# One PSUM pool with banks handed out in turn, and two reorderings around the norms, in a two-layer decoder trunk

## The chip, the core and the metric

The kernel runs on one core of a Trainium2 chip. The metric is the device time of one execution in microseconds (us). The core has five engines with a queue each: TensorE (PE, matmuls and transposes), VectorE (DVE), ScalarE (ACT), GpSimd (POOL) and SyncE (SP, which here issues the loads). Matmuls write to PSUM, which has eight banks of 128 x 512 f32; the other engines read the results from there. Each engine runs its instructions in the order of its queue.

## What is computed

The reference is a decoder trunk of two layers on x of 256 tokens by 1024 features, batch 1, all in f32:

```python
for i in range(DEPTH):
    h = rmsnorm(x, norm_mix[i])
    if i % 2 == 0:
        x = x + even_mixer(h, ...)   # 8 softmax heads and 16 Mamba-2 SSD heads, one projection in, one out
    else:
        x = x + gdn_mixer(h, ...)    # gated DeltaNet: conv, chunked delta rule, gated norm
    h = rmsnorm(x, norm_ffn[i])
    x = x + conv_ffn(h, ...)         # silu(conv(h @ w_gate) + b) * (h @ w_up) @ w_down
    x = x + per_layer_embedding(x, p[i], ...)  # sigmoid(rmsnorm(x) @ w_gate) * (p @ w_proj)
```

## The kernel before

Everything lies transposed in SBUF: features on the 128 partitions, the 256 tokens along the free axis, so that x is eight tiles of 128 x 256. A projection is made from blocks of 128 x 128 weights. `piece` (L133) loads 128 x 1024 weights (512 KB) through four buffers and splits them into a high half `whi` (ACT, L163) and a low half `wlo` (DVE, L164), each with four buffers of its own. `mm3` (L183) then runs three fp32r matmuls per block (L188 to L190): high times high, high times low, low times high. Activations are split likewise: `norm_tile` makes the halves `xx` of a tile of x (`split`, L217 on ACT and L218 on DVE) and the square of the tile (L241 on ACT), which POOL adds up to `nss` (L248). `norm_end` reduces the squares over the partitions on PE (`nps`, L255 and L256), turns them into 1/sqrt by a chain of eleven small DVE instructions (`st` L258, then `rsqrt`), and PE replicates the result over the partitions (`rep`, L270).

The stages follow each other: `even` (to about 192 us), `ffn(0)` with its per-layer embedding `ple` (to 402), `odd` (to 704), `ffn(1)` with its `ple` (to the end). The names in the rows: `pdt`, `pxbc`, `pz`, `pqk`, `pv` are projections of even, `pwa` its output projection; `rows`, `pxT`, `pyT` and the tiles `E` belong to the eight tiles of its SSD heads (function `ssd`), each of which takes on ACT six passes over 128 x 128 (L532 to L534, two heads) and two exponentials over 128 x 384 (L535). `pss` (L569) collects the sums of squares of q and k over the four passes of `qk`, and is read once, at L582. `psc` and `ppT` belong to its softmax heads, `pzs` to its group norm. `pg`, `pu`, `pd` are the FFN's projections, `pgt` the gate of `ple`, whose result `pleg` is made on DVE (L353, L355), ACT (tanh, L354) and added to x (L356). `pab` is odd's first projection, `pgd` its conv projections. For each of its eight key heads odd runs `prep` (a chain of small matmuls and copies: `rows`, `pS`, six times `pY` and `pST`, then `pR`, `pC` twice) and `core` (from `py0` on), while `pgd`, `pvT` and `pz` of other heads stand between them.

The Tile framework orders the instructions: each gets a priority by its place in the program, `high_priority(offset)` moves the ones inside it ahead by so many places, and a scheduler with its own durations sets each engine's queue by these and by when operands and buffers are there. The weight splits have an offset of 80 (`AHEAD`).

Of the eight PSUM banks one belongs to the pool `nrm` for the whole program. The other seven are opened stage by stage as a pool (`psum`, L114): `even` has 3 banks for `acc`, 2 for `ssd` and 2 for `att`; an FFN has 7 for `acc`; `odd` has 3 for `acc`, 1 for `core`, 2 for `prep0`, 1 for `prep1`. A tile of a kind gets a buffer of its kind, and the pool of the next stage is opened when that of the last is closed: the first tile of the new one waits until all of the old one's tiles have been read.

Of the kernel before, what the change touches and what calls it, by code (L numbers as in the profile page):

```python
# [7 lines left out]
F32 = mybir.dt.float32  # L8
# [4 lines left out]
ALU = mybir.AluOpType  # L13
# [3 lines left out]
P = 128  # L17
BLK = 1024
WARM = 30
WO = 7  # L20
AHEAD = 80
KICK = 2
T = 256
D = 1024
# [27 lines left out]
class Trunk:  # L52
    def __init__(self, ctx, tc, stream, xT, pT, pv, tok, cst, out):
        self.tc, self.nc, self.ctx = tc, tc.nc, ctx
        self.stream, self.out = stream, out
        self.off = 0
        self.order = []
        self.n = 0
        self.pshare, self.share = 0.0, 0.0
        nc = self.nc  # L60
        ep = ctx.enter_context
        self.cpool = ep(tc.tile_pool(name="cpool", bufs=1))
        self.rawp = ep(tc.tile_pool(name="rawp", bufs=4))
        self.splp = ep(tc.tile_pool(name="splp", bufs=4))
        self.smallp = ep(tc.tile_pool(name="smallp", bufs=3))
        self.chain = ""
        self.nrm = ep(tc.tile_pool(name="nrm", bufs=1, space=PSUM))

        self.xx = self.moving(self.cpool, 2 * KD, "xx")
        warm = self.cpool.tile([P, 1], F32, tag="warm", name="warm")  # L70
        nc.vector.memset(warm, 0.0)
        nc.scalar.activation(warm, warm, AF.Exp)

        zt = self.cpool.tile([P, 256], F16, tag="zt", name="zt")
        nc.vector.memset(zt, 0.0)
        pz = self.nrm.tile([P, 512], F32, tag="nrm", name="pwarm")
        for _ in range(WARM):
            nc.tensor.matmul(pz[:, :T], zt[:, :P], zt, start=True, stop=True)
        self.pv = self.cpool.tile([P, NPV], F32, tag="pv", name="pv")
        nc.scalar.dma_start(self.pv, pv)  # L80
        xs = self.cpool.tile([P, KD, T], F32, tag="x", name="x")
        for m in range(0, KD, 2):
            nc.sync.dma_start(xs[:, m:m + 2], xT[:, m:m + 2])
        self.x = [xs[:, m] for m in range(KD)]
        self.tok = self.cpool.tile([P, 64], F32, tag="tok", name="tok")
        self.cst = self.cpool.tile([P, NCC], F32, tag="cst", name="cst")
        self.cst_src, self.tok_src = cst, tok
        self.pT = pT
        self.ones = self.cpool.tile([P, 1], F32, tag="ones", name="ones")
        nc.gpsimd.memset(self.ones, 1.0)  # L90
        self.ident = self.c("ident")
        self.id16 = self.cpool.tile([P, P], F16, tag="id16", name="id16")
        self.zb = [[self.cpool.tile([P, 4, P], F16, tag=f"zb{s}_{l}", name=f"zb{s}_{l}") for l in range(6)]
                   for s in range(1)]
# [19 lines left out]
    @contextmanager  # L114
    def psum(self, **banks):

        assert sum(banks.values()) <= 7
        with self.tc.tile_pool(name=self.uid("psum"), bufs=1, space=PSUM) as pool:
            self.psp, self.banks = pool, banks
            yield  # L120

    def acc(self, s="acc"):
        return self.psp.tile([P, 512], F32, tag="acc", name=self.uid(s), bufs=self.banks["acc"])

    def sm(self, s="sm"):
        if self.chain in self.banks:
            return self.psp.tile([P, 512], F32, tag=self.chain, name=self.uid(s), bufs=self.banks[self.chain])
        return self.nrm.tile([P, 512], F32, tag="nrm", name=self.uid(s))

    def small(self, n, s="st", dt=F32):  # L130
# [79 lines left out]
    def split(self, src, hi, lo, scale=None):  # L210

        nc = self.nc
        if scale is None:
            nc.scalar.activation(hi, src, AF.Copy)
            nc.vector.tensor_tensor(lo, src, hi.bitcast(F32), op=ALU.subtract)
        else:
            nc.scalar.activation(hi, src, AF.Copy, scale=scale)  # L217
            nc.vector.scalar_tensor_tensor(out=lo, in0=src, scalar=scale, in1=hi.bitcast(F32),  # L218
                                           op0=ALU.mult, op1=ALU.subtract)


    def norm_begin(self, gain, pool=None):
# [28 lines left out]
    def norm_end(self):  # L251
# [3 lines left out]
            nc.tensor.matmul(ps[:, c:c + 1], self.nss[:, c * P:(c + 1) * P], self.ones, start=True, stop=False)  # L255
            nc.tensor.matmul(ps[:, c:c + 1], self.nlast[:, c * P:(c + 1) * P], self.ones, start=False, stop=True)  # L256
        t = self.small(2)
        nc.vector.tensor_scalar(out=t, in0=ps[:, 0:2], scalar1=1.0 / D, scalar2=EPS, op0=ALU.mult, op1=ALU.add)  # L258
        r = self.cpool.tile([P, 2], F32, tag="rtok", name=self.uid("rtok"), bufs=2)
        self.rsqrt(t, 2, r)  # L260
        self.r = r
# [79 lines left out]
    def ple(self, i, nxt, pool):  # L341
# [4 lines left out]
        for m0 in range(0, KD, 2):  # L346
            ws = self.piece([("ple_w_gate", i, 0, KD, (m0 + j) * P, P) for j in range(2)])
            for j in range(2):
                m = m0 + j
                ps = self.acc("pgt")  # L350
                self.mm3(ps[:, :T], ws[j], a)
                g = pool.tile([P, T], F32, tag="pleg", name=self.uid("pleg"), bufs=4)
                nc.vector.tensor_tensor(g, ps[:, :T], self.R, op=ALU.mult)  # L353
                nc.scalar.activation(g, g, AF.Tanh, scale=0.5)  # L354
                nc.vector.scalar_tensor_tensor(out=g, in0=g, scalar=1.0, in1=self.pp[m], op0=ALU.add, op1=ALU.mult)  # L355
                nc.vector.tensor_tensor(self.x[m], self.x[m], g, op=ALU.add)  # L356
                if nxt:
                    self.norm_tile(m)
                else:
                    nc.sync.dma_start(self.out[:, m], self.x[m])  # L360
        if nxt:
            self.norm_end()

# [789 lines left out]
```

## Time and profile before

| | |
|---|---|
| time, three runs | 919.47, 921.43, 921.58 us (median 921.43) |
| the profiled execution's own time, its span | 923.28 us, 921.5 us |
| PE busy | 900.1 us, 98% |
| PE weight loads | 860.1 us, 93% |
| DVE busy | 747.3 us, 81% |
| ACT busy | 584.8 us, 63% |
| POOL busy | 42.9 us, 5% |
| mean granted PE clock | 0.992 of full speed |

The span is the time from the first to the last instruction that the profiler saw, the time of the execution stands a little above it. PE is busy nearly all the time, so PE's idle time and its clock are what is left to look at. Full speed is 2.4 GHz; a granted clock of 0.5 is the lower of the two levels, 1.2 GHz.

### The profile page before, as it was taken

Reading aid. Unit: us, or ns where it says so; the run is one execution under the profiler, and the core shown is the slowest. Engines: PE = TensorE matmul, PEld = TensorE weight load, DVE = VectorE, ACT = ScalarE, POOL = GpSimd, SP = SyncE. Lnnn points to the kernel's source line nnn. Section 1 sums busy time; section 2 is a strip of 40 time slices with the busy share of each in tenths; the row PEclk is TensorE's granted clock in tenths of the full one; section 3 lists DMA queues with packets and bytes.
Section 4 is the critical chain, followed back from the end, with each engine's and each line's share of the span. In section 5 each row is a group of like instructions: output and inputs, shape, how many; then the busy total and the mean of one; then the engine's idle time right before and its main releaser. Section 6 shows DMA issues by size and latency. Waiting matters only on the chain. (4 is left out here: it accounts for less than half of the span.)

```text
span 921.5 us, 19977 instructions
## 1 busy us (share of the span) xinstructions
PE 900.1 (98%) x7834; PEld 860.1 (93%) x7834; DVE 747.3 (81%) x1662; ACT 584.8 (63%) x1237; POOL 42.9 (5%) x53
## 2 busy tenths in 40 slices
PE   8999999999999999999989999999999999999997
PEld 6988778999999999989889999999999999999997
DVE  6977778988888767789979998999868888876665
ACT  6577555667565545667678778787755665554552
POOL 0000112110000001010000000000002000000100
PEclk9999999999999999999989999999999999999999
DMA  7534332466666566545413333432345666666571
GB/s 276 181 122 131 93 114 92 140 197 193 203 186 197 177 203 209 169 138 158 141 47 93 114 100 108 119 113 88 122 134 177 184 194 199 190 193 189 179 227 48
DMA packets 40990, 141.40 MB, mean 153 GB/s; under 512 B 4672, under 2 KB 6208, under 8 KB 40896
## 3 DMA queue, kind: packets, MB, share of 16 engines
q1 hardware_dynamic: 40608, 139.84, 48.6%
q8 instruction: 61, 1.00, 0.4%
q10 hardware_dynamic: 288, 0.29, 0.1%
q14 instruction: 33, 0.27, 0.1%
HBM read 139.06 MB, written 1.05 MB: 152 GB/s over the span
## 5 line engine op out<-in xcount | busy, mean ns | idle before, releaser
L163 ACT ACTIVATE whi<-raw 128x1024 fp32r<-128x1024 f32 (+2 forms) x266 | 277.7, 1044 | 176.8 <-PE pd L189 38.6
L164 DVE TENSOR_TENSOR wlo<-raw,whi 128x1024 fp32r<-128x1024 f32 (+2 forms) x266 | 319.8, 1202 | 81.8 <-ACT whi L163 79.7
L188 PE MATMUL pg<-xx,whi 128*128 128x256 f32 x352 | 97.4, 277 | 0.6 <-DVE x L703 0.3
L188 PE MATMUL pu<-xx,whi 128*128 128x256 f32 x352 | 97.5, 277 | 0.0
L189 PE MATMUL pg<-xx,whi 128*128 128x256 f32 x352 | 97.4, 277 | 0.0
L189 PE MATMUL pu<-xx,whi 128*128 128x256 f32 x352 | 97.4, 277 | 0.0
L190 PE MATMUL pu<-xx,wlo 128*128 128x256 f32 x352 | 97.4, 277 | 0.0
L190 PE MATMUL pg<-xx,wlo 128*128 128x256 f32 x352 | 97.2, 276 | 0.0
L188 PE MATMUL pd<-yy,whi 128*128 128x256 f32 x352 | 97.2, 276 | 0.0
L189 PE MATMUL pd<-yy,whi 128*128 128x256 f32 x352 | 97.2, 276 | 0.0
L190 PE MATMUL pd<-yy,wlo 128*128 128x256 f32 x352 | 97.2, 276 | 0.0
L188 PE MATMUL pgd<-xx,whi 128*128 128x256 f32 x256 | 76.1, 297 | 0.4 <-DVE z L989 0.4
L190 PE MATMUL pgd<-xx,wlo 128*128 128x256 f32 x256 | 75.0, 293 | 0.0
L189 PE MATMUL pgd<-xx,whi 128*128 128x256 f32 x256 | 74.8, 292 | 0.0
L188 PEld LDWEIGHTS pg<-xx,whi 128*128 128x128 f32 x352 | 66.1, 188 | 0.8 <-issue 0.8
L188 PEld LDWEIGHTS pu<-xx,whi 128*128 128x128 f32 x352 | 66.1, 188 | 0.0
L189 PEld LDWEIGHTS pu<-xx,whi 128*128 128x128 f32 x352 | 66.1, 188 | 0.0
L190 PEld LDWEIGHTS pu<-xx,wlo 128*128 128x128 f32 x352 | 66.1, 188 | 0.0
L189 PEld LDWEIGHTS pg<-xx,whi 128*128 128x128 f32 x352 | 66.1, 188 | 0.0
L190 PEld LDWEIGHTS pg<-xx,wlo 128*128 128x128 f32 x352 | 66.1, 188 | 0.0
L188 PEld LDWEIGHTS pd<-yy,whi 128*128 128x128 f32 x352 | 66.1, 188 | 0.0
L189 PEld LDWEIGHTS pd<-yy,whi 128*128 128x128 f32 x352 | 66.1, 188 | 0.0
(357 smaller groups left out, 2636.1 us busy)
## 6 DMA issues: line engine op xcount, KB each, us to landing
raw<-stream SPq DMA_DIRECT2D x232, 512.0 KB, 3.6
raw<-stream SPq DMA_DIRECT2D x32, 448.0 KB, 3.3
x<-xT SPq DMA_DIRECT2D x4, 256.0 KB, 4.9
out<-x SPq DMA_DIRECT2D x8, 128.0 KB, 1.9
cst<-cst SPq DMA_DIRECT2D x1, 645.0 KB, 7.1
raw<-pT SPq DMA_DIRECT2D x2, 256.0 KB, 2.5
pv<-pv ACTq DMA_DIRECT2D x1, 215.5 KB, 4.4
raw<-stream SPq DMA_DIRECT2D x1, 128.0 KB, 2.0
```

What stands on the lines that cost most here:

```text
L163: nc.scalar.activation(hi, raw[:, :cols], AF.Copy)
L164: self.lo_engine(lo).tensor_tensor(lo_, raw[:, :cols], hi.bitcast(F32), op=ALU.subtract)
L188: nc.tensor.matmul(out, wh, ah, start=start and k == 0, stop=False)
L189: nc.tensor.matmul(out, wh, al, start=False, stop=False)
L190: nc.tensor.matmul(out, wl, ah, start=False, stop=stop and k == n - 1)
```

## The change

It has three parts. One pool `banks` of seven tiles, `bank0` to `bank6`, is kept for the whole program. `psum` now gives each kind of tile a list of banks, those least recently handed out first, and `bank` hands a kind's banks out in strict turn. In `ple`, what follows the gate matmuls of the last two tiles (m = 6, 7) is put into a `high_priority` of 400, `LAST`. In `norm_end` the instruction `st` is issued only after the last low half of an `xx` tile (`lastlo`).

```diff
@@ -19,6 +19,7 @@
 WARM = 30
 WO = 7
 AHEAD = 80
+LAST = 400
 KICK = 2
 T = 256
 D = 1024
@@ -65,6 +66,8 @@
         self.smallp = ep(tc.tile_pool(name="smallp", bufs=3))
         self.chain = ""
         self.nrm = ep(tc.tile_pool(name="nrm", bufs=1, space=PSUM))
+        self.psp = ep(tc.tile_pool(name="banks", bufs=1, space=PSUM))
+        self.used = [0] * 7
 
         self.xx = self.moving(self.cpool, 2 * KD, "xx")
         warm = self.cpool.tile([P, 1], F32, tag="warm", name="warm")
@@ -114,17 +117,25 @@
     @contextmanager
     def psum(self, **banks):
 
+        free = sorted(range(7), key=lambda b: self.used[b])
         assert sum(banks.values()) <= 7
-        with self.tc.tile_pool(name=self.uid("psum"), bufs=1, space=PSUM) as pool:
-            self.psp, self.banks = pool, banks
-            yield
+        self.banks = {}
+        for kind, n in banks.items():
+            self.banks[kind], free = free[:n], free[n:]
+        yield
+
+    def bank(self, kind, s):
+        b = self.banks[kind].pop(0)
+        self.banks[kind].append(b)
+        self.used[b] = self.n
+        return self.psp.tile([P, 512], F32, tag=f"bank{b}", name=self.uid(s))
 
     def acc(self, s="acc"):
-        return self.psp.tile([P, 512], F32, tag="acc", name=self.uid(s), bufs=self.banks["acc"])
+        return self.bank("acc", s)
 
     def sm(self, s="sm"):
         if self.chain in self.banks:
-            return self.psp.tile([P, 512], F32, tag=self.chain, name=self.uid(s), bufs=self.banks[self.chain])
+            return self.bank(self.chain, s)
         return self.nrm.tile([P, 512], F32, tag="nrm", name=self.uid(s))
 
     def small(self, n, s="st", dt=F32):
@@ -215,8 +226,8 @@
             nc.vector.tensor_tensor(lo, src, hi.bitcast(F32), op=ALU.subtract)
         else:
             nc.scalar.activation(hi, src, AF.Copy, scale=scale)
-            nc.vector.scalar_tensor_tensor(out=lo, in0=src, scalar=scale, in1=hi.bitcast(F32),
-                                           op0=ALU.mult, op1=ALU.subtract)
+            self.lastlo = nc.vector.scalar_tensor_tensor(out=lo, in0=src, scalar=scale, in1=hi.bitcast(F32),
+                                                         op0=ALU.mult, op1=ALU.subtract)
 
 
     def norm_begin(self, gain, pool=None):
@@ -255,7 +266,8 @@
             nc.tensor.matmul(ps[:, c:c + 1], self.nss[:, c * P:(c + 1) * P], self.ones, start=True, stop=False)
             nc.tensor.matmul(ps[:, c:c + 1], self.nlast[:, c * P:(c + 1) * P], self.ones, start=False, stop=True)
         t = self.small(2)
-        nc.vector.tensor_scalar(out=t, in0=ps[:, 0:2], scalar1=1.0 / D, scalar2=EPS, op0=ALU.mult, op1=ALU.add)
+        with self.tc.issue_after(self.lastlo.ins):
+            nc.vector.tensor_scalar(out=t, in0=ps[:, 0:2], scalar1=1.0 / D, scalar2=EPS, op0=ALU.mult, op1=ALU.add)
         r = self.cpool.tile([P, 2], F32, tag="rtok", name=self.uid("rtok"), bufs=2)
         self.rsqrt(t, 2, r)
         self.r = r
@@ -349,15 +361,16 @@
                 m = m0 + j
                 ps = self.acc("pgt")
                 self.mm3(ps[:, :T], ws[j], a)
-                g = pool.tile([P, T], F32, tag="pleg", name=self.uid("pleg"), bufs=4)
-                nc.vector.tensor_tensor(g, ps[:, :T], self.R, op=ALU.mult)
-                nc.scalar.activation(g, g, AF.Tanh, scale=0.5)
-                nc.vector.scalar_tensor_tensor(out=g, in0=g, scalar=1.0, in1=self.pp[m], op0=ALU.add, op1=ALU.mult)
-                nc.vector.tensor_tensor(self.x[m], self.x[m], g, op=ALU.add)
-                if nxt:
-                    self.norm_tile(m)
-                else:
-                    nc.sync.dma_start(self.out[:, m], self.x[m])
+                with self.tc.high_priority(offset=LAST if m >= KD - 2 else 0):
+                    g = pool.tile([P, T], F32, tag="pleg", name=self.uid("pleg"), bufs=4)
+                    nc.vector.tensor_tensor(g, ps[:, :T], self.R, op=ALU.mult)
+                    nc.scalar.activation(g, g, AF.Tanh, scale=0.5)
+                    nc.vector.scalar_tensor_tensor(out=g, in0=g, scalar=1.0, in1=self.pp[m], op0=ALU.add, op1=ALU.mult)
+                    nc.vector.tensor_tensor(self.x[m], self.x[m], g, op=ALU.add)
+                    if nxt:
+                        self.norm_tile(m)
+                    else:
+                        nc.sync.dma_start(self.out[:, m], self.x[m])
         if nxt:
             self.norm_end()
 
```

The numbers behind a name tell one tile from another; a line of "..." leaves out rows that repeat the one above them or the one below. The rows of the changed kernel have its own line numbers, 3 to 13 higher.

First place: PE in the even layer, around the `rows` of the second ssd tile. Before, they stand in the middle of the `pxbc` matmuls, one tile ahead of that tile's `pyT`:

```order
L188 MATMUL pxbc_161_815<-xx_1_70,whi_154_775 128x256
L415 MATMUL rows_144_739<-cst_115,ac_69_313 128x128 x2
L538 MATMUL pyT_141_721<-E_142_722,xd_140_719 64x256
L539 MATMUL pyT_141_721<-E_142_722,xd_140_719 64x128
L415 MATMUL rows_144_739<-cst_115,ac_69_313 128x128 x2
L189 MATMUL pxbc_161_815<-xx_1_70,whi_154_775 128x256
...
L523 MATMUL pxT_145_744<-cst_115,xbc1_124_633 128x128 x2
...
L190 MATMUL pqk_172_863<-xx_1_70,wlo_168_854 128x256
L538 MATMUL pyT_147_749<-E_148_750,xd_146_747 64x256
L539 MATMUL pyT_147_749<-E_148_750,xd_146_747 64x128
```

Now the same tile's `rows` and `pyT` (its names are `rows_143` and `pyT_146`) stand behind the last `pss`, among the `pv` matmuls:

```order
L201 MATMUL pqk_254_1322<-xx_1_73,wlo_250_1288 128x256
L620 MATMUL pv_292_1464<-whi_295_1468,xx_1_73 128x512
...
L582 MATMUL pss_108_552<-cst_118,sqk_256_1349 128x2 x2
L621 MATMUL pv_293_1465<-whi_295_1468,xx_1_73 128x512
...
L621 MATMUL pv_293_1465<-whi_295_1468,xx_1_73 128x512
L428 MATMUL rows_143_739<-cst_118,ac_68_313 128x128 x4
L622 MATMUL pv_293_1465<-wlo_296_1469,xx_1_73 128x512
...
L621 MATMUL pv_293_1465<-whi_298_1486,xx_1_73 128x512
L551 MATMUL pyT_146_749<-E_147_750,xd_145_747 64x256
L552 MATMUL pyT_146_749<-E_147_750,xd_145_747 64x128
L428 MATMUL rows_183_953<-cst_118,ac_68_313 128x128 x4
L551 MATMUL pyT_146_749<-E_148_758,xd_145_747 64x256
```

With them the same instructions of ssd tiles 2 to 7 have moved behind the last `pss`; 37 `pv` matmuls are left behind `rows_143`, of 48.

Second place: PE at the start of `odd`. Before, `pab` (24 matmuls) meets the first `nps` after 13 of them, and all the rest but three stand ahead of the first `pgd`:

```order
L190 MATMUL pab_1004_5463<-xx_1_70,wlo_1003_5460 32x256
L188 MATMUL pab_1004_5463<-xx_1_70,whi_1002_5459 32x256
L255 MATMUL nps_982_5409<-ones_116,nss_978_5373 128x1
L189 MATMUL pab_1004_5463<-xx_1_70,whi_1002_5459 32x256
```

Now 18 stand ahead of the first `nps`, and `pgd` follows behind the next one:

```order
L200 MATMUL pab_1001_5455<-xx_1_73,whi_999_5451 32x256
L201 MATMUL pab_1001_5455<-xx_1_73,wlo_1000_5452 32x256
L266 MATMUL nps_980_5405<-ones_119,nss_976_5369 128x1
L199 MATMUL pab_1001_5455<-xx_1_73,whi_999_5451 32x256
L199 MATMUL pgd_1039_5560<-xx_1_73,whi_1033_5549 128x256
```

The first matmul of `pab` follows the last `pgt` in both.

Third place: PE in `odd`, the end of the first head's chain (`pR`, `pC`) and the start of `core` (`py0`) and of the next `prep` (`pS`). Before, six and six `pgd` matmuls stand around the second `pR`, two behind the last `pC`, and none between `py0` and `pS`:

```order
L892 MATMUL pR_1101_5851<-nid_998_5451,id16_118 128x512
L189 MATMUL pgd_1321_6817<-xx_1_70,whi_1314_6805 128x256
...
L188 MATMUL pgd_1321_6817<-xx_1_70,whi_1314_6805 128x256
L899 MATMUL pR_1101_5851<-S32_1097_5832,L32_1077_5701 128x128 x4
L189 MATMUL pgd_1321_6817<-xx_1_70,whi_1314_6805 128x256
...
L904 MATMUL pC_1103_5859<-R16_1102_5857,T16_1082_5719 128x128
L189 MATMUL pgd_1321_6817<-xx_1_70,whi_1314_6805 128x256
L190 MATMUL pgd_1321_6817<-xx_1_70,wlo_1315_6806 128x256
L928 MATMUL py0_1216_6414<-bv_1203_6331,S32_1097_5832 128x128
L856 MATMUL pS_1165_6104<-id16_118,T16_1163_6101 128x128
```

Now the second `pR` runs without `pgd` in front, four stand behind it with `pvT`, and two, `rows` and three more lie ahead of `py0` and `pS`:

```order
L905 MATMUL pR_1098_5843<-nid_995_5443,id16_121 128x512
L912 MATMUL pR_1098_5843<-S32_1094_5824,L32_1074_5693 128x128 x4
L931 MATMUL pvT_1212_6401<-cst_118,v2_1207_6365 128x128 x2
L199 MATMUL pgd_1324_6850<-xx_1_73,whi_1314_6803 128x256
...
L199 MATMUL pgd_1324_6850<-xx_1_73,whi_1314_6803 128x256
L917 MATMUL pC_1100_5851<-R16_1099_5849,T16_1079_5711 128x128
...
L201 MATMUL pgd_1324_6850<-xx_1_73,wlo_1315_6804 128x256
L428 MATMUL rows_1281_6625<-cst_118,gc_1025_5532 128x128 x4
L199 MATMUL pgd_1324_6850<-xx_1_73,whi_1314_6803 128x256
...
L941 MATMUL py0_1213_6406<-bv_1200_6323,S32_1094_5824 128x128 x2
L869 MATMUL pS_1162_6096<-id16_121,T16_1160_6093 128x128
```

What moved is the fill between the steps of the chain, not the steps.

## Rows read from the trace of the kernel before

**Rows 1.** The page, busy us, share of the span, instructions.

```profile
PE 900.1 (98%) x7834; PEld 860.1 (93%) x7834; DVE 747.3 (81%) x1662; ACT 584.8 (63%) x1237; POOL 42.9 (5%) x53
```

**Rows 2.** PE's waits, whole span: us in total, times, longest.

```profile
PE pab L188 <- DVE pleg L353: 2.0, 1, 2.0
PE pS L856 <- DVE T L852: 2.0, 1, 2.0
PE rep L270 <- DVE ry L206: 1.4, 1, 1.4
...
PE pwa L188 <- DVE ri L196: 1.0, 1, 1.0
...
PE py L928 <- DVE S L905: 0.5, 1, 0.5
...
PE pvT L918 <- DVE v L384: 0.3, 1, 0.3
PE pg L188 <- DVE x L703: 0.3, 1, 0.3
...
PE nps L255 <- POOL nss L248: 0.3, 1, 0.3
```

**Rows 3.** Windows: busy us of PE, PEld, DVE, ACT, POOL; granted clock; DMA.

```profile
100.00:110.00 10.00, 10.00 (x54) 7.09 (x54) 8.09 (x24) 8.40 (x23) 0.95 (x1) 1.00 0.36 107
162.00:164.00 2.00, 2.00 (x19) 1.97 (x18) 1.95 (x4) 2.00 (x5) 0.00 (x0) 1.00 0.60 236
404.00:406.00 2.00, 1.76 (x11) 1.52 (x12) 2.00 (x4) 1.12 (x3) 0.58 (x1) 0.69 0.62 221
406.00:408.00 2.00, 2.00 (x12) 1.71 (x11) 1.62 (x6) 0.68 (x2) 0.15 (x1) 0.50 0.65 164
408.00:410.00 2.00, 2.00 (x19) 1.95 (x18) 0.16 (x1) 1.64 (x3) 0.00 (x0) 0.96 0.25 102
464.00:466.00 2.00, 2.00 (x19) 1.82 (x18) 1.44 (x5) 1.17 (x4) 0.00 (x0) 0.50 0.48 193
466.00:468.00 2.00, 2.00 (x13) 1.91 (x13) 0.39 (x2) 1.43 (x5) 0.00 (x0) 0.50 0.00 0
468.00:470.00 2.00, 2.00 (x16) 1.91 (x16) 1.05 (x4) 1.27 (x5) 0.00 (x0) 0.60 0.00 0
```

**Rows 4.** Timeline, 401 to 406: start, us, engine, line, tile, idle before.

```profile
401.95 0.28 PE L190 MATMUL pgt<-xp,wlo 128*128 128x256 f32 x1
...
402.47 0.95 DVE L218 SCALAR_TENSOR_TENSOR xx<-x,pv,xx 128x256 fp32r<-128x256 f32 x1
...
404.24 0.28 PE L188 MATMUL pab<-xx,whi 128*32 128x256 f32 x1 [2.01 <-DVE pleg L353]
...
404.36 0.28 PE L189 MATMUL pab<-xx,whi 128*32 128x256 f32 x1
...
405.42 0.73 POOL L248 TENSOR_TENSOR nss<-nss,nsq 128x256 f32<-128x256 f32 x1 [2.28 <-ACT nsq L241]
```

**Rows 5.** Timeline of PE, 100 to 106.

```profile
100.29 0.60 PE L415 MATMUL rows<-cst,ac 128*128 128x128 f32 x4
100.73 0.38 PE L523 MATMUL pxT<-cst,xbc 128*128 128x128 f32 x2
...
101.65 0.39 PE L607 MATMUL pv<-whi,xx 128*128 128x512 f32 x1
101.88 0.39 PE L608 MATMUL pv<-whi,xx 128*128 128x512 f32 x1
...
104.81 0.65 PE L538 MATMUL pyT<-E,xd 128*64 128x256 f32 x2
...
105.60 0.44 PE L523 MATMUL pxT<-cst,xbc 128*128 128x128 f32 x2
```

**Rows 6.** Lines of ACT, 40 to 155: busy, mean ns, idle before.

```profile
L163 ACT ACTIVATE whi<-raw 128x1024 fp32r<-128x1024 f32 x25 | 26.6, 1063 | 18.8 <-PE pqk L189 9.2 <-PE pv L608 5.3 <-PE pxbc L189 3.3
L535 ACT ACTIVATE E<-E 128x384 f32<-128x384 f32 x16 | 8.5, 530 | 0.1
...
L532 ACT ACTIVATE E<-rows,ac 128x128 f32<-128x128 f32 x16 | 5.9, 372 | 0.3 <-PE rows L415 0.2
```

## The prediction

> **What bounds the kernel now.** I read the page's busy shares first: TensorE (PE) is busy for 900.1 of the span's 921.5 us [rows 1]. So only two things can move the time: the some 20 us in which PE idles, and the stretches in which its granted clock is under 1. The amount of matmul work is the same before and after. Next come PE's waits [rows 2]: two of them are 2 us long, and both lie in the odd layer. The windows [rows 3] then show that each of these two holes is followed by a stretch at half the granted clock (0.50, the lower of its two levels, 1.2 GHz). That is a second price as large as the hole itself. The timeline shows who is late at the first hole [rows 4], and what PE and ScalarE (ACT) spend on one ssd tile in the even layer [rows 5, 6], where the change moves most instructions.
>
> My sum is made against the profiled execution's 923.28 us, 1.85 above the median 921.43 of the runs shown. I take the difference as it comes out and put it to the median. A measurement of this kernel tells 0.3%, or 2.8 us, from no change.
>
> **The start of odd (the pab matmuls).** The last pgt matmul starts at 401.95, and pab's first one at 404.24 [rows 4]: PE idles 2.0 us [rows 2] until VectorE (DVE) has read the old pool's last bank, because the new pool is opened as a whole. Then the clock drops: 2 us at 0.69, 2 at 0.50, 2 at 0.96 [rows 3] lose 2 x (0.31 + 0.50 + 0.04) = 1.7 us. Together 3.7 us. With banks handed over singly, pab's bank was read long ago. The order says that 18 pab matmuls (six of eight input tiles) now come first, some 0.118 us apart (404.24, 404.36 [rows 4]): PE is then busy from 402.1 to 404.2, and stands next at the first nps matmul, which needs the running sum of squares with tile 6. Before, that sum ended at 405.42 + 0.73 = 406.15 [rows 4]. In the new order tile 6's x add stands one 0.33 us instruction earlier on DVE, and its tanh ahead of the older tile's square on ACT, so about 405.8. A stall of 1.6 us replaces the hole. LAST does not bring more, since the 1.2 us weight split still stands ahead of m 7's chain in DVE's order. Does a 1.6 us stall drop the clock? The nearest rows are the 1.4 of rep [rows 2], which ends at 160.6 and after which the window from 162 still shows 1.00 [rows 3], and the 2.0 above. 1.6 is nearer to 1.4, so I take 3.7 - 1.6 = **2.0 gained**, and 0.4 for the bound where the clock drops all the same. The st instruction behind the last low half costs nothing here: that half (0.95 us beside a POOL add [rows 4]) no longer stands between st and the rest of the rsqrt, and PE has pgd matmuls to run, the wait for xx 7 being the longer one.
>
> **Middle of odd (455 to 470).** The holes py 0.5, pS 2.0 and pvT 0.3 [rows 2] come to 2.8 us, and the clock behind them loses 2 x (0.50 + 0.50 + 0.40) = 2.8 us in three windows [rows 3]. The two prep banks are now in strict turn, and the scheduler lays the same pgd fill differently: less between pR and pC, and some with rows and pvT ahead of py0 and pS. The chain pR, ACT copy, pC, DVE add is unchanged and there is as much fill, so I leave the idle time at 2.8 us, but in pieces of 0.4 to 1.2 us by the lengths of the steps. None reaches 1.4, so no clock drop: **2.8 gained**, with bounds of 0 (the clock still falls) and 4 (part of the idle goes too). Later a turn of the prep chain (pS to pY) has no fill left: **0.6 lost** (0 to 1.0), my estimate: two of the shorter waits of 0.3 [rows 2].
>
> **Even layer, ssd (45 to 118).** Here the turn costs something that the diff does not say. The tile pss is taken from the att kind and stays alive until all four qk passes have written it. Of the two att banks, round-robin gives every second rows tile pss's bank, so the rows of ssd tile 1 wait until pss was read, and with them, in order, everything of ssd tiles 1 to 7: rows, the E passes, pyT. Before, they lay among pxbc and pqk matmuls. Now they come behind the last pss, among the 37 pv matmuls left. Between two tiles' pyT PE has its own work of rows 0.44 (100.29 to 100.73), pxT about 0.26, two heads of pyT 1.58 (104.81 to 105.60 is one), four pv at 0.23 [rows 5]: 3.2 us. ACT needs six passes of about 0.37 and two of 0.53 [rows 6], 3.3 us by durations (they overlap, so some less). That is a near balance, where before PE was busy for 10.00 of 10 us [rows 3]. The first pyT also waits for rows, ACT and a DVE product in a row with a weight split (1.06 us [rows 6]) in front, about 1 us. I take 1.0 + 0.4 + five tiles at 0.15 = **2.2 lost**. The bounds are 0 (pv covers all) and 6 (each tile waits for a split of 1.06 too).
>
> **Attention and the group norm (118 to 168).** With its fill used up earlier, attention has some 88 pz matmuls to hide its softmax chains in where it had 133. I charge four waits like those that a chain leaves elsewhere (0.3 to 0.5 [rows 2]): **1.5 lost** (0 to 4). In return a block of 24 matmuls (2.8 us) now stands between the group norm's pzs and its rep, which idled 1.4 [rows 2]: **1.0 gained** (0 to 1.4). The pwa wait of 1.0 stays.
>
> **Stage changes to the two FFNs.** pg's waits of 0.3 for the first x and nps's 0.3 [rows 2] lie where nps and rep now come after 12 and 23 of the new stage's matmuls, not after 7 and 9: **0.9 gained** over both (0 to 1.6). DMAs, weight splits and their order on the SP queue are unchanged, and cost nothing.
>
> Sum: -2.0 - 2.8 + 0.6 + 2.2 + 1.5 - 1.0 - 0.9 = -2.4, so 923.28 becomes 920.9 and the median **919.0 us**.
>
> **Rivals.**
> *Stalls take the holes' place.* PE meets nps at 404.2 and the shorter stalls at 460 add up, and the clock falls to half as before. For it: the half clock follows both 2 us holes, and 1.6 lies between the rows. Against it: after 1.4 it did not fall. Then the two gains shrink to 0.4 and 0, the sum is +2.0, and the time 923.4. The Trainium skill (TensorE: Matmul & The Clock Gate, section "A second HAM failure mode: psum-queue depth-cycling") speaks for it: cycling through PSUM banks gave short idles between groups of matmuls, over which the clock swung. By that rule the time would be this case's 923.4, by the rows alone 919.0; no row of before shows whether short idles in a row do this here.
>
> *The squeezed ssd becomes the bound (slower).* Place: PE between the last pqk and the first psc, 100 to 118. If pz's weight splits (1.06 us [rows 6]) fall among the E passes, ACT has 4.4 us a tile against PE's 3.2. Five tiles then cost 1.2 each, with 1.0 for the first: 7.0 instead of 2.2. One of these stalls reaching 2 us brings a clock dip of 1.7 as at 402. The sum is then -2.4 + 4.8 + 1.7 = +4.1, or 925.5. It decides from some 5.2 us lost there above the 2.2 (for +2.8). For it: both engines are near balance. Against: the E passes overlap, and DVE (8.09 of 10 busy) and ACT (8.40) had room in the same stretch [rows 3].
>
> *Everything is covered.* ssd and attention stalls hide behind pv and pz, both clock drops and some of the idle go, and 1.0 of the 3.7 lost there is left: -2.0 - 4.0 - 1.0 - 0.9 + 0.6 + 1.0 = -6.3, or 915.1.
>
> **How the numbers follow.** Forecast 0.40, stalls in the holes' place 0.27, ssd the bound 0.19, everything covered 0.14. The forecast's 919.0 lies just inside 0.3%, so I give half of it (0.21) to faster and 0.19 to same. The second case is same but for 0.03 slower. So faster 0.21 + 0.14 = 0.35, same 0.19 + 0.24 = 0.43, slower 0.19 + 0.03 = 0.22. The forecast alone holds from 916.5 to 921.5. The range that leaves out one in five takes in nearly all of the two outer cases: 914.5 to 925.5.
>
> **What would show it.** Right: pab's wait is gone from PE's waits and nps has one of about 1.6; the windows from 404 to 410 and from 462 to 470 show a granted clock of 1.00; PE idles some 2 us between 100 and 118, under pyT; rep waits 0.4 or less. Wrong: a window at 0.50 behind nps or in the middle of odd (the second case), more than 5 us of idle in front of pyT (the third), or DVE late with cg in the pxbc stretches, which now run back to back at 0.118 us a matmul.

## The result and the profile after

Four executions of the changed kernel took 925.98, 926.89, 928.12 and 929.84 us, median 927.5; the kernel before, on the same chip, 921.12. The ratio is 1.0071 [1.0056, 1.0086]: slower, 8.5 us above the forecast and outside its range. The same program in a later job (`e3_after_again`) gave 1.0028 [1.0006, 1.0049]: its executions fall into two groups some 7 us apart, so the text gives the spread of the runs with each median.

The page of the profiled execution (925.98 us, span 924.2) beside [rows 1]: PE is busy 3.6 us longer for the same 7834 matmuls, though its mean granted clock rose from 0.992 to 0.997.

```profile
PE 903.7 (98%) x7834; PEld 864.3 (94%) x7834; DVE 746.4 (81%) x1662; ACT 584.5 (63%) x1237; POOL 44.3 (5%) x53
```

So I read where the time is by landmarks. The tile view of both kernels: min/median/max ns, first to last start. Before:

```profile
L188 PE MATMUL pg<-xx,whi x352: 276/276/357, 192.3 to 824.1; 128*128 128x256 f32 x176
L188 PE MATMUL pab<-xx,whi x8: 276/412/418, 404.2 to 410.1; 128*32 128x256 f32 x8
L188 PE MATMUL pwo<-gm,whi x128: 276/281/367, 643.1 to 704.8; 128*128 128x256 f32 x128
L188 PE MATMUL pgt<-xp,whi x128: 276/276/364, 379.5 to 916.2; 128*128 128x256 f32 x128
```

After:

```profile
L199 PE MATMUL pg<-xx,whi x352: 276/279/366, 195.9 to 827.6; 128*128 128x256 f32 x176
L199 PE MATMUL pab<-xx,whi x8: 276/276/283, 413.4 to 420.0; 128*32 128x256 f32 x8
L199 PE MATMUL pwo<-gm,whi x128: 276/276/387, 650.1 to 708.2; 128*128 128x256 f32 x128
L199 PE MATMUL pgt<-xp,whi x128: 276/276/364, 390.2 to 918.9; 128*128 128x256 f32 x128
```

From the start to the first pg (even): +3.6. From there to the first pab (the first FFN with its embedding): 211.9 to 217.5, +5.6. From pab to the last pwo (odd): 300.6 to 294.8, -5.8. From there to the last pgt (the second FFN): -0.7. Together +2.7, the difference of the spans. The first FFN is where nothing was predicted; and since the kernel before had the hole of 2.0 us in front of pab in this stage, the rest of it grew by more than 5.6. Windows in the middle of each FFN show what it is (columns as in [rows 3]). Before:

```profile
240.00:300.00 60.00, 60.00 (x532) 60.00 (x531) 48.62 (x78) 35.68 (x56) 0.00 (x0) 1.00 0.62 195
760.00:820.00 60.00, 60.00 (x532) 60.00 (x531) 48.76 (x78) 35.72 (x56) 0.00 (x0) 1.00 0.64 192
```

After:

```profile
240.00:300.00 60.00, 60.00 (x511) 60.00 (x511) 46.83 (x75) 34.73 (x53) 0.00 (x0) 1.00 0.61 186
760.00:820.00 60.00, 60.00 (x532) 60.00 (x531) 48.76 (x78) 35.73 (x56) 0.00 (x0) 1.00 0.63 193
```

PE never idles in any of them, and the granted clock is 1.00 in all four. Yet in 60 us the first FFN of the changed kernel gets through 511 matmuls, the other three through 532. By the starts of the matmuls one follows the other after 113.3 ns in the one case, 117.8 in the other; in the changed kernel's first FFN 1,742 of 1,814 such steps are of the slow kind, 7.8 us more than at 113.3, and 7.3 more than the same steps take in the kernel before. I call this the **pace**. It is not the clock, and not a wait that the profile shows.

The kernel before has both paces too. These windows lie in the gate matmuls (pgt) of the first and of the second layer, again with PE busy throughout and a clock of 1.00. Before:

```profile
384.00:400.00 16.00, 16.00 (x143) 16.00 (x143) 14.13 (x27) 11.10 (x23) 3.50 (x4) 1.00 0.47 157
898.00:914.00 16.00, 16.00 (x138) 16.00 (x137) 11.23 (x23) 5.36 (x9) 0.00 (x0) 1.00 0.17 60
```

After:

```profile
395.00:411.00 16.00, 16.00 (x139) 16.00 (x138) 14.03 (x27) 10.70 (x22) 3.57 (x4) 1.00 0.51 149
901.00:917.00 16.00, 16.00 (x144) 16.00 (x143) 11.78 (x23) 5.59 (x10) 0.00 (x0) 1.00 0.19 68
```

The fast pace in the second of these is the 0.7 us that the second FFN gained. In odd, the kernel before has 254 of 323 steps of pwo at the slow pace (the median of 281 ns above shows it), the changed one 54 of 325.

PE's waits after, beside [rows 2]:

```profile
PE rep L282 <- DVE ry L217: 1.7, 2, 1.4
PE nps L266 <- POOL nss L259: 1.6, 2, 1.4
...
PE pwa L199 <- DVE x L709: 1.2, 1, 1.2
...
PE rep L282 <- DVE rtok L217: 1.0, 4, 0.3
PE pST L895 <- ACT S L890: 1.0, 1, 1.0
...
PE pz L201 <- DVE wlo L175: 0.7, 1, 0.7
```

pab and pS are gone from it; nps has one of 1.4. The windows at these places, and three of even:

```profile
8.00:13.00 5.00, 4.19 (x33) 3.27 (x34) 4.37 (x11) 5.00 (x13) 0.00 (x0) 1.00 1.02 382
100.00:110.00 10.00, 10.00 (x54) 6.38 (x52) 5.25 (x12) 7.28 (x24) 0.00 (x0) 1.00 0.01 2
160.00:170.00 10.00, 7.56 (x49) 7.35 (x50) 9.32 (x26) 3.96 (x8) 2.53 (x3) 0.83 0.49 156
414.00:416.00 2.00, 1.66 (x15) 1.31 (x13) 2.00 (x4) 1.61 (x4) 0.39 (x2) 1.00 0.71 205
416.00:418.00 2.00, 0.94 (x8) 0.94 (x9) 1.97 (x4) 0.11 (x1) 1.00 (x1) 1.00 0.49 111
418.00:420.00 2.00, 2.00 (x20) 1.98 (x19) 1.25 (x7) 1.81 (x3) 0.00 (x0) 1.00 0.57 227
465.00:467.00 2.00, 1.03 (x17) 0.57 (x12) 2.00 (x7) 1.57 (x3) 0.00 (x0) 1.00 0.71 172
467.00:469.00 2.00, 0.68 (x6) 0.44 (x6) 1.58 (x5) 1.04 (x3) 0.00 (x0) 1.00 0.93 311
469.00:471.00 2.00, 2.00 (x18) 1.83 (x19) 2.00 (x4) 1.46 (x4) 0.00 (x0) 1.00 0.34 137
```

In odd the clock stays at 1.00 behind both stalls, where [rows 3] had 0.69 and 0.50. In even it fell for a part of 160 to 170, behind the group norm's rep (1.4) and pwa (1.2). The kernel before fell in even as well, but near the start; its window from 8:

```profile
8.00:13.00 5.00, 4.16 (x23) 2.69 (x24) 3.88 (x9) 4.92 (x12) 0.00 (x0) 0.66 1.01 372
```

By the granted clock each of the two falls costs 1.7 us, so the clock is no part of the 3.6 by which even is longer. Where those 3.6 us are is seen in the tile view of psc (first of the softmax heads) and pws (last of even). Before:

```profile
L626 PE MATMUL psc<-kT,qT x16: 272/322/373, 118.2 to 143.4; 64*128 64x128 f32 x16
L188 PE MATMUL pws<-am,whi x64: 276/276/387, 168.8 to 190.9; 128*128 128x256 f32 x64
```

After:

```profile
L639 PE MATMUL psc<-kT,qT x16: 272/322/373, 116.8 to 136.2; 64*128 64x128 f32 x16
L199 PE MATMUL pws<-am,whi x64: 281/281/364, 172.1 to 195.0; 128*128 128x256 f32 x64
```

Up to psc the changed kernel is 1.4 us ahead. From psc to pws it takes 55.3 us, not 50.6.

### The profile page after: what moved, and what is told of

Same layout as the page of the kernel before. It is cut to its first block, busy times and chain, and to the rows that moved or that the text cites. A ratio compares the mean times of both kernels' runs of the same rounds, so it can differ in the third digit from the quotient of the medians.

```text
span 924.2 us, 19981 instructions
## 1 busy us (share of the span) xinstructions
PE 903.7 (98%) x7834; PEld 864.3 (94%) x7834; DVE 746.4 (81%) x1662; ACT 584.5 (63%) x1237; POOL 44.3 (5%) x53
## 4 chain that ended last, share of the span: by engine, by line
PE 87%; DVE 7%; ACT 4%; issue 2%; DMA 1%; POOL 0%; ACTq 0%; POOLq 0%; DVEq 0%
PE pg L199 4%; PE pg L200 4%; PE pd L200 4%; PE pd L201 4%; PE pd L199 4%; PE pg L201 4%; PE pu L200 4%; PE pu L201 4%; PE pu L199 4%; PE pgd L199 3%; PE pgd L200 3%; PE pgd L201 3%; DVE wlo L175 3%; PE pz L200 2%; PE pz L201 2%; PE pz L199 2%
## 5 line engine op out<-in xcount | busy, mean ns | idle before, releaser
L199 PEld LDWEIGHTS pd<-yy,whi 128*128 128x128 f32 x352 | 66.8, 190 | 0.0
L201 PEld LDWEIGHTS pd<-yy,wlo 128*128 128x128 f32 x352 | 66.1, 188 | 0.0
```

Source lines behind the costliest of these rows:

```text
L199: nc.tensor.matmul(out, wh, ah, start=start and k == 0, stop=False)
L201: nc.tensor.matmul(out, wl, ah, start=False, stop=stop and k == n - 1)
```

## Experiments

Medians stand beside that of the kernel before in the same job (920.75, 921.55, 920.95, 921.01 and 921.33 us in the five). Diffs are against the changed kernel unless the text says otherwise; "banks in turn" is the change's `bank`, "old pools" the stage-wise pools of before.

### What sets the pace

My first theory was that PE enters a stream of matmuls at one of two paces and keeps it, and that weight tiles shifted in SBUF (`lead` in `ffn`: the weights of f = 2 and 3 start 16, 32 or 48 elements further) reset it. The rival was the banks in turn themselves.

**e1_tick0** puts eight 1-column matmuls, whose result nobody reads, into the first FFN:

```diff
+                if i == 0 and f == 1:
+                    self.tick()
```

> The changed kernel, with eight matmuls of 128x1 (on constants, read by nobody) put on PE behind the second block row (f = 1) of the first FFN. Pace theory: in the changed kernel the 1,742 matmuls of the first FFN run 118 ns apart where before they ran 113.3 apart; the pace is set where a stream of fp32r matmuls starts again after other work on PE, and then kept. Then the eight matmuls make it be set anew: behind them either 113.3 for the rest of the FFN (about 6.7 us saved, 921 us) or 118 again (927.5, +0.5 for the eight). Bank theory: the new order of PSUM banks makes the pace of this FFN slow; then 118 before and behind the eight, 928. Ssd theory: the loss lies in the even layer alone; then nothing changes, 928.

922.51, ten runs from 920.0 to 933.5. The profiled execution (920.61) is slow before and behind the eight matmuls and turns to 113 ns behind the shifted tiles; its window from 240 has 532 matmuls. In this execution the small matmuls do nothing; the shifted tiles can turn the pace. Here they turned it from slow to fast in both FFNs, in the changed kernel's first FFN they left it slow.

**e1_nokick** takes the shifts away:

```diff
-                                lead={KICK: (0, 16), KICK + 1: (32, 48)}.get(f, (0, 0)))
+                                lead=(0, 0))
```

> The changed kernel, with the weight tiles of f = 2 and 3 of both FFNs at the same offset as all others (lead always 0). Pace theory: the pace is kept from the last restart (the two rep transposes in f = 0), so the first FFN stays at 118 ns throughout, and only the slow stretches of f = 2 and 3 in the second FFN go (some 0.4 us): 927. Rival to it, that the shifted tiles set the pace: then the first FFN changes pace against the changed kernel at f = 2, to 113.3 (about 920.5), or the second one goes slow (934).

Median 929.89, six runs from 918.4 to 933.7; the profile (925.53) has the first FFN slow, the second fast. **e2_before_nokick**, the same edit in the kernel before:

> The kernel before, with the weight tiles of f = 2 and 3 at the same offset as all others. In the kernel before rep finds its operand ready. Wait theory: the pace is then fixed at 113.3 ns with or without the shifted tiles; the 3 x 24 matmuls at 118 to 120 ns per FFN go, 0.8 us in all: 920.0, one cluster. If it is the shifted tiles that keep the FFNs fast: clusters at 927 and 934 appear.

920.0: six runs at 919.5 to 921.1, two at 927.5. With the shifts, none of some 100 runs of the kernel before is above 923.6. So by its times it can have an upper group too, and the shifts seem to keep it out. Neither of the two was profiled, and their mean clock is lower as well (0.993, against 0.994 to 0.996 in the other six), so the pace is likely there, not shown.

**e3_kick2** shifts the weights of f = 6 and 7 as well:

```diff
-                                lead={KICK: (0, 16), KICK + 1: (32, 48)}.get(f, (0, 0)))
+                                lead={KICK: (0, 16), KICK + 1: (32, 48), 6: (0, 32), 7: (16, 48)}.get(f, (0, 0)))
```

> The changed kernel, with weight tiles at other offsets a second time, in f = 6 and 7, in the order 0, 32, 16, 48. It costs some 0.4 us in each FFN. Pace theory: the order of instructions and the banks are the same, and a second disturbance can turn a slow FFN fast (or a fast one slow), so the pace of the first FFN changes at f = 6 or 7 in the trace, and the runs at 927 become fewer, with a cluster at 919 to 922. Bank theory: nothing but the 0.8 us, 928.

931.3 (930.1 to 932.3), 1.011 [1.0096, 1.0125]: the slowest of all, and now steadily. By the starts of its matmuls the first FFN runs at 113.3 ns up to f = 6 and slow from these tiles on; the second likewise. Its windows:

```profile
240.00:300.00 60.00, 60.00 (x511) 60.00 (x511) 47.04 (x75) 33.72 (x52) 0.00 (x0) 1.00 0.57 187
760.00:820.00 60.00, 60.00 (x512) 60.00 (x511) 46.97 (x75) 34.40 (x54) 0.00 (x0) 1.00 0.60 190
```

The banks and their order are those of the changed kernel, in which the second FFN was fast. So a change of the weights' places alone can set the pace. That the banks in turn are not needed for it this run doesn't show, since it has them; the kernel before shows it, whose pgt matmuls of the second layer are slow in an old pool. Over the 18 profiled executions pgt is slow in 17 of 36 cases, in FFNs with old pools in 7 of 12. The rival falls.

### What in the change brings it on

**e1_pool**: the banks in turn alone, without `LAST` and the place of `st`.

```diff
-        with self.tc.issue_after(self.lastlo.ins):
-            nc.vector.tensor_scalar(out=t, ...)
+        nc.vector.tensor_scalar(out=t, ...)
...
-                with self.tc.high_priority(offset=LAST if m >= KD - 2 else 0):
```

> The one pool with banks in turn alone: no LAST priority, st not held back. Pool theory: all that moved in the profile (ssd behind pss, pab early, the fill of odd) comes from the pool, so even takes 194.8 us as in the changed kernel and the wait of pab is gone; 927.5 if the first FFN draws 118 ns, 920.5 if it draws 113.3. If LAST and st matter: the wait at the start of odd is 1 us or more longer than the changed kernel's 1.4.

923.68, six runs at 921.1 to 924.1 and four at 929.1 to 930.0; 1.0048 [1.0021, 1.0075]. The mixture is there without the two reorderings.

**e2_hold** tests another suspect. In the changed kernel a weight split stands in the middle of the rsqrt chain before the first FFN's rep (timeline of DVE after; in brackets the idle time before):

```profile
199.70 0.16 DVE L217 SCALAR_TENSOR_TENSOR ry<-rt,ry 128x2 f32<-128x2 f32 x1
200.59 1.23 DVE L175 TENSOR_TENSOR wlo<-raw,whi 128x1024 fp32r<-128x1024 f32 x1 [0.73 <-ACT whi L174]
201.73 0.15 DVE L215 SCALAR_TENSOR_TENSOR rt<-ry 128x2 f32<-128x2 f32 x1
201.92 0.16 DVE L216 TENSOR_TENSOR rt<-rt,st 128x2 f32<-128x2 f32 x1
202.12 0.16 DVE L217 SCALAR_TENSOR_TENSOR rtok<-rt,ry 128x2 f32<-128x2 f32 x1
```

so that rep waits 0.25 us in a running stream. `hold` issues the low halves of f = 1 and 2 behind the chain:

```diff
+                with self.tc.issue_after(hold.ins) if hold else ExitStack():
+                    self.lo_engine(lo).tensor_tensor(lo_, raw[:, :cols], hi.bitcast(F32), op=ALU.subtract)
...
+                                hold=hold if f in (1, 2) else None)
```

> The changed kernel, with the weight splits' low halves of f = 1 and 2 of both FFNs issued on DVE behind the last instruction of the norm's rsqrt chain, so that no 1.2 us split stands in the middle of it. The two rep transposes then come after 11 pu matmuls and find their operand ready, where in the changed kernel they waited 0.2 to 0.3 us. Wait theory: the pace of the 1,584 matmuls behind rep is left to chance only where rep had to wait; now no execution has an FFN at 118 ns, all runs lie within 918 to 922, median 919.5. If the wait has nothing to do with it: the runs keep two or three clusters some 7 us apart (920, 927, 934), median near 927.

925.15 (923.1 to 927.2). rep does not wait any more, and the first FFN is slow all the same, 511 matmuls from 240 to 300, and here already ahead of rep: the suspect falls.

**e4_entry** gives the FFN its banks in another rotation, so that PE's order at its start is nearly that of before and rep has no wait:

```diff
+        if banks == {"acc": 7}:
+            free = free[-1:] + free[:-1]
```

> The changed kernel, with each FFN's first bank taken as the one used last, not first. PE's order at the start of both FFNs is then nearly that of the kernel before: behind nps come 17 pg and 9 pu matmuls, then rep with its operand ready, and no weight split stands in the rsqrt chain; only five pu matmuls more stand ahead. All else is the changed kernel. Entry theory: the order at the FFN's start decides whether the pace is left to chance; then all runs lie at 917.5 to 921 with both FFNs at 113.3 ns. If something ahead of it (even with banks in turn) decides: runs at 925 to 929 remain.

Seven runs at 917.7 to 919.6, five at 924.6 to 929.5. The mixture stays, so the order at the start alone doesn't decide either.

**e3_after_again** runs the changed kernel itself again.

> The changed kernel itself, run again. Chance theory: in each FFN rep restarts PE's stream after a wait, and the pace behind it is a draw; in the eleven such restarts traced so far three stayed at 118 ns behind the shifted tiles. Then about half of the executions have both FFNs fast, at 918 to 921, most of the rest one slow, at 925 to 929. Fixed theory: the first FFN of this kernel always comes out slow, as in its four runs so far; all runs at 925 to 930.

Twelve runs: seven at 919.2 to 923.5, five at 925.7 to 928.5. With the first four, nine of 16 lie in the upper group. The execution profiled here (928.51) has the first FFN slow, 511 matmuls. Of the changed kernel no execution of the lower group was profiled; that those have the fast pace is inferred from the distance of some 7 us and from `e4_entry`, whose profiled run (918.15) has 531 and 532.

The groups are not the clock's. Each run is recorded with its mean granted clock; as an estimate, take span x (1 - clock) as lost to it and subtract that. The changed kernel's 16 runs then lie at 914.7 to 916.2 (seven) and 921.1 to 923.2 (nine), and 99 runs of the kernel before in one group, 912.7 to 916.0 with a median of 914.6. The clock's loss is 3.5 us in the mean of the 16, 4.8 in that of the 99.

In one place this execution differs from the first profiled one, though the program is the same: the clock falls in the middle of odd, where it had stayed.

```profile
466.00:468.00 2.00, 0.85 (x10) 0.43 (x7) 1.57 (x5) 1.30 (x3) 0.00 (x0) 0.89 0.83 270
468.00:470.00 2.00, 1.82 (x8) 1.82 (x9) 2.00 (x5) 0.63 (x1) 0.00 (x0) 0.50 0.38 147
...
472.00:474.00 2.00, 2.00 (x10) 2.00 (x11) 1.98 (x5) 0.59 (x3) 0.00 (x0) 0.50 0.61 223
```

### Even

**e1_pss** tests the prediction's mechanism: pss's bank is taken out of att's turn until pss is read.

```diff
+        held = self.banks["att"].pop()
...
+        self.banks["att"].append(held)
```

> The changed kernel, with the bank of pss taken out of the att kind's turn until pss has been read. Ssd theory: ssd's tiles lie among the pxbc and pqk matmuls again, even takes 191 to 192.5 us in place of 194.8, the time is 2.5 to 3.5 us less (924.5). Pace theory: that too, but the pace of the first FFN is drawn anew since everything ahead of it has moved: 924.5 at 118 ns, 917.5 at 113.3.

926.8; ten runs from 921.0 to 939.4 and one of 4982, which I leave out. Nothing is won. The profiled execution is the one of 939.38, with both FFNs slow. Its even stage can be read all the same: ssd is laid out as before, and the first psc starts at 118.2, as before; but po waits 2.2 and pzs 1.8, the clock falls at both places, and the first pg starts at 200.6. So what even loses lies behind ssd, and in this execution giving ssd its old place does not bring it back.

**e5_even_turn** has banks in turn in even alone, and old pools after it, with `LAST` and `st`; **e3_no_pool** has old pools throughout, with `LAST` and `st`. The core of the first:

```diff
+            self.turn = "ssd" in banks
+            if not self.turn:
+                self.banks = banks
```

> The changed kernel, with banks in turn in the even stage alone; the FFNs and odd have pools of their own, as before (LAST and st as in the changed kernel). PE's order in both FFNs is that of the kernel before. Even theory: the even stage by itself takes 194 to 195 us, not 191, and leaves the pace of the first FFN to chance, so the runs are a mixture, about half at 919.5 to 922 and half some 7 us above. If the FFN's own banks or order are needed for the slow pace: one cluster at 919.5 to 922.

> The kernel before with LAST and st behind the last low half, and the old pools. In both FFNs PE's order around nps and rep is that of the kernel before. If these two parts cost or bring something by themselves: the wait of pab at the start of odd changes from 2.0 us. Pool theory: it stays within 0.5 us of 2.0, odd stays at 300 us, the time within 1.5 us of 921, one cluster.

922.36 (12 runs, 921.0 to 924.6; 1.0011 [1.0001, 1.0021]) against 917.51 (916.4 to 918.8; 0.9957 [0.9943, 0.9971]). The first pg starts at 195.7 and at 192.2. The profiled executions (922.42 and 918.76) are 3.6 apart at the last pgt as well. So banks in turn cost even 3.5 us; the clock falls once in even in both executions. They do not make the first FFN slow by themselves: `e5_even_turn` has 532 in both windows, and its times are one group.

### Odd and the best version

**e2_hybrid0** goes the other way: even in a pool of its own, banks in turn from the first FFN on.

```diff
         self.even()
+        self.psp = self.ctx.enter_context(self.tc.tile_pool(name="banks", bufs=1, space=PSUM))
+        self.used = [0] * 7
```

> The changed kernel with the even stage in a pool of its own, as before, and the one pool of banks in turn from the first FFN on. In the first FFN rep then stands after 9 pu matmuls with no split in the chain, as before; in the second FFN chain and rep are those of the changed kernel. Wait theory: only the second FFN draws its pace, so the runs fall into two clusters, some 7 us apart, and none has both slow. Even takes 191 to 192 us as before, not 194.8; the lower cluster at 915 to 918, the upper one at 922 to 925. If the banks in turn make an FFN slow: both FFNs vary still, three clusters.

917.54 (915.2 to 919.6), 0.9949 [0.9934, 0.9964]. Here nps still waits 2.0 us at the start of odd, and the clock falls:

```profile
404.00:406.00 2.00, 0.95 (x9) 0.94 (x10) 1.97 (x4) 0.11 (x1) 1.00 (x1) 1.00 0.41 98
406.00:408.00 2.00, 2.00 (x16) 2.00 (x13) 0.98 (x5) 1.81 (x3) 0.00 (x0) 0.68 0.56 223
408.00:410.00 2.00, 2.00 (x10) 1.91 (x11) 1.36 (x9) 0.51 (x2) 0.00 (x0) 0.50 0.00 0
```

**e2_hyhold** adds `hold` to it.

> Both of the above: even in its own pool, banks in turn from the first FFN on, and the splits of f = 1 and 2 behind the rsqrt chain. Wait theory: neither FFN draws, all runs lie in one cluster at 915 to 918, some 3 us or more below the kernel before. If not: clusters 7 us apart remain.

**914.79 us (913.6 to 916.5), 0.9921 [0.9909, 0.9934]**: faster than both kernels. PE is busy 893.9 us, and behind nearly the same wait at nps (1.93 us, against 1.96 in `e2_hybrid0`) the clock stays:

```profile
404.00:406.00 2.00, 0.56 (x5) 0.22 (x3) 2.00 (x5) 1.12 (x3) 0.62 (x1) 1.00 0.80 231
406.00:408.00 2.00, 1.51 (x13) 1.49 (x14) 1.91 (x6) 0.39 (x2) 0.44 (x1) 1.00 0.55 133
408.00:410.00 2.00, 2.00 (x20) 1.98 (x19) 1.21 (x6) 1.93 (x4) 0.00 (x0) 1.00 0.37 150
...
240.00:300.00 60.00, 60.00 (x531) 60.00 (x531) 48.77 (x78) 35.58 (x55) 0.00 (x0) 1.00 0.60 194
```

**e3_hybrid_plain** is `e2_hyhold` without `LAST` and `st`.

> The fastest kernel so far (even in its own pool, then banks in turn, splits behind the chain: 914.8 us) without LAST and without st held back. Pool theory: what is left of the 6.8 us against the kernel before comes from the banks in turn at the start and in the middle of odd, so 914 to 916.5. If LAST or st carries the gain: 918 or more.

919.01 (six runs at 917.8 to 920.8, one at 926.9): 4.2 us are lost again (4.8 by the distances to the kernel before of the same job), the clock falls at both places of odd.

**e4_before_st** and **e4_before_last** have the kernel before with one of the two reorderings:

> The kernel before with st held back behind the last low half, and nothing else (LAST and st together without the pool took 917.5 against 920.95). If st carries it: 917.5, with odd at 296 to 297 us and no window at half clock between 455 and 475. If LAST carries it: 921 and odd at 300 to 301.

> The kernel before with LAST, and nothing else. If LAST carries the gain of the two: 917.5, odd at 296 to 297. If st does: 921, odd at 300 to 301. If only both together do (by the fill of odd's chains being laid out in another way): 921 here and there.

917.31 (916.8 to 917.7; 0.9959 [0.9946, 0.9972]) and 918.09 (917.8 to 919.6; 0.9971 [0.9959, 0.9982]); together (`e3_no_pool`) they bring no more. With `st` alone pab waits 1.5, and the windows that were at 0.69 and 0.50 in [rows 3] are at 1.00, as is the one from 464:

```profile
404.00:406.00 2.00, 1.71 (x15) 1.34 (x14) 1.94 (x4) 0.33 (x2) 0.73 (x1) 1.00 0.47 117
406.00:408.00 2.00, 2.00 (x20) 1.98 (x19) 1.24 (x6) 1.92 (x3) 0.00 (x0) 1.00 0.55 209
...
464.00:466.00 2.00, 2.00 (x25) 1.84 (x25) 1.69 (x6) 1.89 (x6) 0.00 (x0) 1.00 0.06 25
```

With `LAST` alone pab still waits 2.3, and the clock is at 1.00 too. By the estimate of above they lose 0.9 and 1.7 us to the clock in the mean of their four and six runs, the kernel before 4.8, and what is left of the span, 915 us, is that of the kernel before. So the gain of both lies in the clock.

## Why the prediction was wrong

**Start of odd: right.** Forecast: pab's wait gone, 1.6 at nps, no fall of the clock, 2.0 gained (3.7 - 1.6 is 2.1, a slip of 0.1). Measured: gone, 1.4, and 1.00. But that the clock held is in part luck, since "1.6 is nearer to 1.4" is not how it goes. Behind waits of 1.93 to 1.96 at nps it fell in `e2_hybrid0` and `e3_hybrid_plain`, and held in `e2_hyhold`, `e4_entry` and the changed kernel's second profile; behind 2.36 at pab it fell in `e3_no_pool`, behind 2.35 it held in `e4_before_last`.

**Middle of odd: right in one execution of two.** The idle time stays (2 x 2.00 - 1.03 - 0.68 = 2.3 us from 465 to 469), in pieces of at most 1.0. In the first profile the clock does not fall behind it, and odd is 5.8 us shorter to the last pwo, of which 5.1 are the clock's two falls of before. In `e3_after_again`, with the same order, it falls again, and odd is 3.0 longer than in the first. So the order of the fill alone does not decide it, and the 2.8 were not a sure gain. `e1_pool` has the dip too (0.72 from 466, 0.50 from 468), the kernel before with `LAST` or `st` alone has not, each in one profile.

**ssd, attention and group norm: the places were wrong.** Under pyT is no idle time: PE is busy 10.00 of 10 us from 100 to 110, and up to psc the changed kernel is 1.4 us ahead, of which 1.7 are the clock's fall at 8; so ssd cost 0.3, not 2.2. Two mechanisms of the text, the squeezed ssd and its rival, fall with that. The loss is in the next term: from psc to pws 4.7, where the sum had 1.5 - 1.0 = 0.5. Of it 1.7 are the clock's fall from 163.9, 1.1 longer waits (pz 0.7 on wlo, po 0.6, pwa 0.1, rep 0.1, less ppT's 0.4 of before), and by the starts of the matmuls some 2 us the pz fill itself. It is cut into 28 runs between the heads' matmuls, before into 14, and where a pz matmul meets one of another kind it takes mostly 0.20 to 0.22 us in place of 0.114. That all three terms together (2.7) come near even's 3.6 is luck. rep's gain of 1.0 did not come: it still waits 1.4.

**Stage changes: the step that failed.** "0.9 gained over both", and "DMAs, weight splits and their order on the SP queue are unchanged, and cost nothing". Instead a split landed in the rsqrt chain, which `e2_hold` shows to be no cause, and the first FFN took 5.6 us longer: 7.3 by pace, less the 2.0 of the hole in front of pab. Without these 7.3 the span would have been 2.7 - 7.3 = 4.6 shorter, against 2.4 predicted. Even that flatters the sum, as the execution profiled before was one of the slowest of its kernel: by the runs, the lower group of `e3_after_again` has a median of 920.4, 0.5 below the kernel before in its job. No term of the sum and no rival had the pace, since "the amount of matmul work is the same before and after" was taken to mean the same time at full clock. The profile of before could have warned: its pgt matmuls of the second layer and most of pwo are slow at a clock of 1.00, and so are the weight tiles of f = 2 and 3, 118 to 120 ns apart.

**LAST and st: wrong.** "LAST does not bring more" and "costs nothing here" hold inside the changed kernel's first hole only. Alone they bring 3.4 us (`e3_no_pool`), by the clock, and with banks in turn from the first FFN on 4.2 to 4.8.

**The rivals.** Stalls with a fall of the clock in the holes' place did not come in the first profile of odd; in the second one came in its middle, as that rival had it. The Trainium skill (TensorE: Matmul & The Clock Gate, section "A second HAM failure mode: psum-queue depth-cycling") would have PE's clock swing from cycling through PSUM banks; here the mean clock rose from 0.992 to 0.997 and is 1.00 throughout both FFNs, whose seven banks are in turn. The trace shows no such swing; but PE has no short idles in these stretches either, so it does not test the rule.

**What stays open.** Shown is that the loss is the pace in one FFN, in two profiles and by their times in nine of 16 executions, and that the slow pace needs no wait at rep, no fall of the clock and no banks in turn. Not settled is what in the changed program brings it on: both groups of times came wherever even and the first FFN both take their banks from the one pool (`e1_pool`, `e3_after_again`, `e4_entry`), and hardly in the eight kernels tried where they don't (`e3_hybrid_plain` one run of seven, `e2_before_nokick` two of eight, the rest none). How PE enters the stream seems to be drawn anew in each execution, and so does whether the clock falls behind a stall; that is a description, not a cause.

## What to carry to other kernels

Count matmuls per window in a long stream before and after a change, not only busy time and clock: a fully busy PE at full clock can still differ by 4%. Test the parts of a change one by one, since here one part brought 3.4 us, another cost 3.5, and their sum hid both. Profile a program more than once before a fall of the clock, or its absence, is put down to a change. Banks in strict turn paid here where stages meet, and cost where they cut the fill of the softmax heads into more pieces; try them per stage.

## What was not expected of the hardware

Back-to-back matmuls of 128 x 128 by 128 x 256 in fp32r have two paces, 113.3 and 117.8 ns, at a granted clock of 1.00 and without idle time. One is kept over 1,700 matmuls, can change at weight tiles that start at shifted places in SBUF (`e3_kick2`: fast to slow in both FFNs), and differs between executions of one program; both occur in the kernel before. And the clock's fall behind a stall does not go by the stall's length: the same wait of 1.93 to 1.96 us at nps had it in two profiles and not in others, and in the changed kernel one execution has the fall in the middle of odd and another has not.
